# A diffusion-transformer block whose first 128 features are modulated, and multiplied, ahead of the next 128

## The chip, the core and the metric

The kernel runs on one core of a Trainium2 chip. The metric is the device time of one execution in microseconds (us). TensorE does the matrix products, VectorE and ScalarE the elementwise work, GpSimd a little of it; SyncE issues most of the loads from memory (HBM) into on-chip memory (SBUF), and products accumulate in PSUM.

## The reference, cut to what matters

One layer: adaptive norm, one combined input projection, four attention mixers, output projection, then the same norm and a SwiGLU. The change touches the way into the input projection alone:

```python
mod = (silu_c @ w_ada[l] + b_ada[l])[:, None, :]        # 2048 -> 6 * 2048
mod_c = silu_cc @ w_ada[l] + b_ada[l]                   # the same for the context
sh_a, sc_a, gt_a, sh_f, sc_f, gt_f = jnp.split(mod, 6, axis=-1)
h = rms_norm(x, g_attn[l]) * (1.0 + sc_a) + sh_a        # 256 latent tokens
hc = rms_norm(xc, g_attn[l]) * (1.0 + csc_a) + csh_a    # 256 context tokens
pl = jnp.split(h @ w_in[l], offsets, axis=-1)           # 2048 -> 4928 columns
pc = jnp.split(hc @ w_in[l], offsets, axis=-1)
```

Everything is float32. Shift and scale of one feature need its two columns of w_ada over all 2048 rows, so 128 features need 2.1 MB of that matrix.

## The kernel before, in words

A float32 product is made of three: each factor is split into a rounded part and the remainder (`whi`, `wlo` for weights, a pair in `hT` for activations), and hi*hi, hi*lo and lo*hi are added up (`mm3s`, L165 to L168). ScalarE writes the rounded part of a weight tile (L142), VectorE the remainder (L145).

The 2048 features are 16 chunks of 128, and two chunks are a "pair". The first part of the projection goes in groups of pairs, `parts = [[0], [1], [2, 3], [4, 5], [6, 7]]`: for a group, the columns of five blocks (queries of two mixers, NA_Q and GQ_Q; then NA_V, GQ_KV, NA_K) are multiplied with that group's features and added to what the groups before gave. So products can start once pair 0 is modulated.

For that, `ada_load` fetches a pair's 256 shift and 256 scale columns, 16 loads of 256 KB in rows of 1 KB, and `ada_pe` multiplies them with silu(c) on TensorE (L301): the left factor is 32 columns wide, and four blocks of 128 features (j = 0 to 3) lie side by side in four column groups of the array. The result is copied (`mvs`, L304), transposed (L307), and biases are added on VectorE (`scg`, `sha`). `modulate` forms h from the normalised, transposed tokens (`xnT`, written by `tokens_T`, transposes at L268) in three steps: h_f (L325), its rounded part on ScalarE (L330), the remainder on VectorE (L331).

The stage's order: tokens 0 and 1 (256 latent tokens) are loaded and normalised; pair 0's loads stand on SyncE's queue with the first weight tiles, NA_Q's two (`raw_q`) between them and GQ_Q's two (`raw_g`) behind; L301 and the eight `tokens_T` share TensorE; the buffers of the latent tokens are then reused for the context tokens, which GpSimd loads (`load_tokens(2)`, `(3)`, L189) when the last transpose has read them. `first_group` multiplies the query blocks, then NA_V and GQ_KV for the latent tokens (`units[:2]`), takes in the context tokens, and goes on with the rest.

Order of the instructions: Tile places each engine's instructions by a simulation of its own in which the earlier in the program goes first among those that are ready, so L301 and L268 alternate. `issue_after` (the helper `after`) adds an order on one engine. Work beside the products (the other pairs' `ada_pe`) is a set of generators in `Side`, stepped by `side.pump(cost)` when the planner's clock `now` has reached their `ready` time. For pair 1 that time is 8.0 from the start of the group.

Of the kernel before, what the change touches and what calls it, by code (L numbers as in the profile page):

```python
# [87 lines left out]
def hybrid_dit_kernel(ctx: ExitStack, tc: tile.TileContext, a, out):  # L88
# [72 lines left out]
    def mm3s(jobs, w_left=False):  # L161


        for dst, l, r, start, stop in jobs:
            pe.matmul(dst, lhsT=l[0], rhs=r[0], start=start, stop=False)  # L165
            pe.matmul(dst, lhsT=l[0 if w_left else 1], rhs=r[1 if w_left else 0], start=False, stop=False)  # L166
        for dst, l, r, start, stop in jobs:
            pe.matmul(dst, lhsT=l[1 if w_left else 0], rhs=r[0 if w_left else 1], start=False, stop=stop)  # L168

    def sub(pair, *sl):  # L170
        return pair[0][sl], pair[1][sl]
# [8 lines left out]
    def tsl(t):  # L180
        return slice(t * P, (t + 1) * P)
# [12 lines left out]
    def ada_load(pr, ks):  # L194
# [9 lines left out]
            raws.append(raw)  # L204
        return raws

    load_tokens(0)
    cc = const.tile([P, 2, KC], F32, name="cc")
    act.dma_start(cc, a["cc"].rearrange("t (p k) -> p t k", k=KC))
# [5 lines left out]


    w_in = a["w_in"]
    raws0 = ada_load(0, range(0, 12, 2))
    raw_q = stream_raw(w_in[0:2 * P, NA_Q:NA_Q + 512].rearrange("(k p) n -> p k n", p=P), [P, 2, 512])
    raws0 += ada_load(0, range(12, KC, 2))  # L220
    raw_g = stream_raw(w_in[0:2 * P, GQ_Q:GQ_Q + 512].rearrange("(k p) n -> p k n", p=P), [P, 2, 512])

    make_identity(nc, ident)
    ones = const.tile([P, 1], F32, name="ones")
# [56 lines left out]
        sp.dma_start(raw, src)  # L281
        return raw

    def ada_pe(pr, raws=None, per=4, wait=0.0):

        mv = misc()
        batches = [range(k, k + 2 * per, 2) for k in range(0, KC, 2 * per)]
        if raws is None:  # L290
            ahead = ada_load(pr, batches[0])
            yield 0.0, wait
        for i, ks in enumerate(batches):
            if raws is None:
                now, ahead = ahead, (ada_load(pr, batches[i + 1]) if i + 1 < len(batches) else None)
            else:
                now = raws[i * per:(i + 1) * per]
            for kc in range(ks[0], ks[0] + 2 * per):
                raw = now[(kc - ks[0]) // 2]
                for j in range(4):  # L300
                    pe.matmul(mv[32 * j:32 * j + 32, :P], lhsT=cs32[:, kc, :], rhs=raw[:, kc % 2, j // 2, tsl(j % 2)], start=(kc == 0), stop=(kc == KC - 1), skip_group_check=True)  # L301
            yield 0.5 * per, wait
# [12 lines left out]
        dve.tensor_tensor(out=scg[:, k2, :], in0=scg[:, k2, :], in1=col(colB[:, k2]), op=ALU.mult)  # L315
        dve.tensor_tensor(out=sha[:, k2, :], in0=cpv[:, 0], in1=col(colA[:, k2]), op=ALU.add)
        yield 0.1, 0.0

    def modulate(pr, ws_=(0, 1)):
        hf = {}  # L320
        for w in ws_:
            hf[w] = sb0.tile([P, 2, S], F32, name="h_f", bufs=2)
            for kk in range(2):
                kc = 2 * pr + kk
                dve.tensor_scalar(out=hf[w][:, kk, :], in0=xnT[pr][:, kk, w * S:(w + 1) * S], scalar1=scg[:, kc, w:w + 1], scalar2=sha[:, kc, w:w + 1], op0=ALU.mult, op1=ALU.add)  # L325
        if ws_[0] == 0:
# [11 lines left out]
        norm_tokens(t)  # L338
    for pr in range(8):
        xnT[pr] = htile(F32)  # L340
    first = ada_pe(0, raws0, 1)
    for _ in range(3):
        next(first)
    for pr in range(8):
        tokens_T(0, pr)
        if 1 < pr < 6:
            next(first)
    load_tokens(2)
    load_tokens(3)
    w_q = split(raw_q, 512)  # L350
    for _ in first:
        pass
    modulate(0, (0,))
    w_g = split(raw_g, 512)


    na_qT = kv.tile([P, 4, S], F32, name="qT", bufs=3)
# [149 lines left out]
            bias.append(b)  # L507

    def first_group():
        q_block([0], True, [w_q])  # L510
        held = {}
        for c0, units in blocks[:3]:
            held[c0] = (w_g if c0 == GQ_Q else stream_w(w_in, 0, c0, 512), units)
            if c0 == blocks[0][0]:
                behind = (newest["act"], newest["dve"])
            one_pair(held[c0], units[:2])
        with after(*behind):
            for t in (2, 3):
                norm_tokens(t)
            tokens_T(1, 0)  # L520
            modulate(0, (1,))
        for c0, units in blocks[1:3]:
            one_pair(held[c0], units[2:])
        for pr in range(1, 8):
            tokens_T(1, pr)
        c0, units = blocks[3]
        one_pair((stream_w(w_in, 0, c0, 512), None), units, True)
# [10 lines left out]
    for gi, prs in enumerate(parts):  # L538
        nxt = []
        if gi + 1 < len(parts):  # L540
            for pr in parts[gi + 1]:
                nxt.append(side.add(ada_pe(pr, wait=(3.0, 1.5, 5.5, 5.5)[gi]), lane="ada", width=1))
                if gi == 0:
                    nxt[-1]["ready"] = side.now + 8.0
        if gi == 2:
            made = prepare()
            gate_tasks = add_ada(2, 7.0, ada_raw, (0, 1))
        if gi == len(parts) - 1:
            keep(*made)
# [693 lines left out]
```

## Time and profile before

| | |
|---|---|
| time, median of 3 runs | 1356.57 us (1356.53 to 1358.23) |
| profiled execution | 1355.29 us, of which the span of its instructions is 1353.5 us |
| mean granted TensorE clock | 0.996 |
| busy: VectorE, ScalarE | 923.2 us (68%), 625.7 us (46%) |
| read from HBM | 314.56 MB, 237 GB/s over the span |

Times in the rows count from the first instruction. Engines are PE (TensorE), PEld (its weight loads), DVE (VectorE), ACT (ScalarE), POOL (GpSimd), SP (SyncE), and a row of a stretch lists them as PE, PEld, DVE, ACT, POOL. L301 is line 301. An arrow "a<-b" between tiles says that a is written from b; "[2.00 <-ACT h L330]" says that the engine sat idle for 2.00 us until that instruction released it. The ends of matrix products are modelled, so the distance between two starts tells their price. A granted clock of 1.00 is 2.4 GHz, 0.50 is 1.2 GHz.

### The profile page before, as it was taken

Reading aid. Unit: us, or ns where it says so; the run is one execution under the profiler, and the core shown is the slowest. Engines: PE = TensorE matmul, PEld = TensorE weight load, DVE = VectorE, ACT = ScalarE, POOL = GpSimd, SP = SyncE. Lnnn points to the kernel's source line nnn. Section 1 sums busy time; section 2 is a strip of 40 time slices with the busy share of each in tenths; the row PEclk is TensorE's granted clock in tenths of the full one; section 3 lists DMA queues with packets and bytes.
Section 4 is the critical chain, followed back from the end, with each engine's and each line's share of the span. In section 5 each row is a group of like instructions: output and inputs, shape, how many; then the busy total and the mean of one; then the engine's idle time right before and its main releaser. Section 6 shows DMA issues by size and latency. Waiting matters only on the chain.

```text
span 1353.5 us, 21027 instructions
## 1 busy us (share of the span) xinstructions
PE 1324.0 (98%) x7018; PEld 1077.5 (80%) x7018; DVE 923.2 (68%) x1687; ACT 625.7 (46%) x1183; POOL 99.6 (7%) x159
## 2 busy tenths in 40 slices
PE   6999999999999999999999999999999999999997
PEld 4788888778886777777888888888888888888886
DVE  4577789998679747778887954445555566556565
ACT  4532343564334435557445444444444444444453
POOL 1110000100000000000322200001001000011000
PEclk9999999999999999999999999999999999999999
DMA  9999996586687756455999855567667655676553
GB/s 367 344 356 323 322 364 220 171 268 213 198 262 262 247 166 212 135 184 164 344 368 340 307 191 192 193 196 219 210 212 228 218 193 185 203 226 224 193 178 129
DMA packets 190161, 322.29 MB, mean 238 GB/s; under 512 B 22466, under 2 KB 62436, under 8 KB 189028
## 3 DMA queue, kind: packets, MB, share of 16 engines
q1 hardware_dynamic: 177568, 285.28, 63.8%
q0 software_dynamic: 9136, 32.53, 6.5%
q10 hardware_dynamic: 3348, 3.13, 0.7%
q8 instruction: 55, 0.90, 0.3%
q14 instruction: 54, 0.44, 0.1%
HBM read 314.56 MB, written 6.31 MB: 237 GB/s over the span
## 4 chain that ended last, share of the span: by engine, by line
PE 68%; DVE 1%; ACT 1%; DMA 0%; issue 0%; POOL 0%; POOLq 0%; DVEq 0%; SPq 0%; ACTq 0%
PE acc L165 21%; PE acc L168 21%; PE acc L166 21%; PE m L862 1%; PE m L607 1%; PE m L861 1%; PE m L913 1%; PE m L897 1%; PE m L658 1%; DVE wlo L145 0%; PE m L165 0%; PE m L166 0%; PE m L168 0%; ACT whi L142 0%; DMA raw<-in_w_out_dram 0%; PE m L385 0%
## 5 line engine op out<-in xcount | busy, mean ns | idle before, releaser
L145 DVE TENSOR_TENSOR wlo<-raw,whi 128x512 fp32r<-128x512 f32 (+1 forms) x764 | 490.4, 680 | 286.0 <-ACT whi L142 281.5
L142 ACT CAST whi<-raw 128x512 fp32r<-128x512 f32 (+1 forms) x764 | 437.6, 615 | 520.2 <-PE acc L166 427.5
L165 PE MATMUL acc<-whi,h_hi 128*128 128x512 f32 x704 | 274.2, 390 | 0.7 <-ACT h_hi L1013 0.7
L166 PE MATMUL acc<-whi,h_lo 128*128 128x512 f32 x704 | 274.1, 389 | 0.4 <-DVE h_lo L1014 0.4
L168 PE MATMUL acc<-wlo,h_hi 128*128 128x512 f32 x704 | 190.8, 390 | 0.0
L165 PE MATMUL acc<-whi,h 128*128 128x512 f32 (+1 forms) x416 | 161.6, 392 | 1.2 <-ACT tok L791 0.5
L166 PE MATMUL acc<-whi,h 128*128 128x512 f32 (+1 forms) x416 | 157.1, 379 | 0.0
L168 PEld LDWEIGHTS acc<-wlo,h_hi 128*128 128x128 f32 x704 | 132.1, 188 | 28.5 <-DVE wlo L145 1.2
L165 PEld LDWEIGHTS acc<-whi,h_hi 128*128 128x128 f32 x704 | 132.2, 188 | 28.2 <-ACT h_hi L1013 1.1
L166 PEld LDWEIGHTS acc<-whi,h_lo 128*128 128x128 f32 x704 | 132.2, 188 | 28.0 <-DVE h_lo L1014 0.7
L165 PE MATMUL acc<-whi,ah 128*128 128x512 f32 (+1 forms) x364 | 139.1, 384 | 0.0
L166 PE MATMUL acc<-whi,al 128*128 128x512 f32 (+1 forms) x364 | 138.6, 382 | 0.0
L380 DVE SCALAR_TENSOR_TENSOR ada_acc<-raw,cs,ada_acc 128x512 f32<-128x512 f32 x135 | 100.9, 747 | 21.7 <-DMA raw<-in_w_ada_dram 20.2
L168 PE MATMUL acc<-wlo,h 128*128 128x512 f32 (+1 forms) x416 | 114.5, 379 | 1.1 <-DVE wlo L145 1.0
L168 PE MATMUL acc<-wlo,ah 128*128 128x512 f32 (+1 forms) x364 | 96.2, 382 | 0.0
L165 PEld LDWEIGHTS acc<-whi,h 128*128 128x128 f32 x416 | 78.0, 188 | 19.2 <-issue 3.7
L166 PEld LDWEIGHTS acc<-whi,h 128*128 128x128 f32 x416 | 78.2, 188 | 13.4 <-issue 1.2
L168 PEld LDWEIGHTS acc<-wlo,h 128*128 128x128 f32 x416 | 75.9, 188 | 16.2 <-DVE wlo L145 2.5
L165 PEld LDWEIGHTS acc<-whi,ah 128*128 128x128 f32 x364 | 68.4, 188 | 13.3
L166 PEld LDWEIGHTS acc<-whi,al 128*128 128x128 f32 x364 | 68.5, 188 | 13.1
L168 PEld LDWEIGHTS acc<-wlo,ah 128*128 128x128 f32 x364 | 67.6, 188 | 13.3
L177 POOL TENSOR_TENSOR rstd<-ms,mhalf 128x1 f32<-128x1 f32 (+2 forms) x24 | 18.1, 755 | 513.5 <-DVE ms L175 513.5
(238 smaller groups left out, 1419.8 us busy)
## 6 DMA issues: line engine op xcount, KB each, us to landing
raw<-in_ffn_wg_dram SPq DMA_DIRECT2D x176, 256.0 KB, 2.8
raw<-in_ffn_wu_dram SPq DMA_DIRECT2D x176, 256.0 KB, 3.5
raw<-in_ffn_wd_dram SPq DMA_DIRECT2D x176, 256.0 KB, 3.7
raw<-in_w_in_dram SPq DMA_DIRECT2D x144, 256.0 KB, 4.7
raw<-in_w_ada_dram SPq DMA_DIRECT2D x144, 256.0 KB, 3.4
araw<-in_w_ada_dram SPq DMA_DIRECT2D x128, 256.0 KB, 5.1
raw<-in_w_out_dram SPq DMA_DIRECT2D x64, 256.0 KB, 3.4
graw<-in_w_ada_dram POOLq DMA_DIRECT2D x32, 512.0 KB, 6.1
```

What stands on the lines that cost most here:

```text
L142: act.copy(hi, raw_)
L145: dve.tensor_tensor(out=lo, in0=raw_, in1=hi.bitcast(F32), op=ALU.subtract)
L165: pe.matmul(dst, lhsT=l[0], rhs=r[0], start=start, stop=False)
L166: pe.matmul(dst, lhsT=l[0 if w_left else 1], rhs=r[1 if w_left else 0], start=False, stop=False)
L168: pe.matmul(dst, lhsT=l[1 if w_left else 0], rhs=r[0 if w_left else 1], start=False, stop=stop)
L177: pool.tensor_tensor(out=r[:, :n], in0=v[:, :n], in1=mhalf[:, :n], op=ALU.pow)
L380: dve.scalar_tensor_tensor(out=acc_, in0=part, scalar=cs[:, 0, kc:kc + 1], in1=acc_, op0=ALU.mult, op1=ALU.add)
L607: pe.transpose(ps[:, tsl(j)], src[:, tsl(j)], ident)
L658: pe.matmul(o[:, :S], lhsT=vt(kc)[:, v0:v0 + P], rhs=pT[:, kc, :], start=(kc == 0), stop=(kc == 3))
L861: pe.matmul(sc, lhsT=ml_qT[:, h, tsl(t)], rhs=ml_kT[:, h, :], start=True, stop=False)
L862: pe.matmul(sc, lhsT=qpeT[hb, h // 2, tsl(t)], rhs=kpeT[hb, :], start=False, stop=True)
L897: pe.matmul(sc, lhsT=df_qT[hb, h, tsl(t)], rhs=df_kT[h // 2][hb, h % 2, :], start=True, stop=True)
```

## The change

Pair 0 is no longer loaded and formed by `ada_load` and `ada_pe`. `ada_load1(kc)` loads shift and scale columns of one chunk of 128 features, in 8 loads of 256 KB with rows of 512 B, and `ada_one(kc)` multiplies them in two column groups (shift, scale). The queue order becomes: 8 loads for chunk 0, its NA_Q and its GQ_Q weight tile, 8 loads for chunk 1, its two tiles. `both_blocks(kc)` multiplies one chunk with NA_Q and GQ_Q for the latent tokens; it is called for chunk 0 ahead of `ada_one(1)` in the program, and for chunk 1 in `first_group`. Chunk 0 is modulated by `modulate1(0)` as soon as its shift and scale are there. In `first_group` the context norms are ordered behind other instructions than before, and pair 1's `ada_pe` gets a later ready time (11.0 for 8.0), a longer first wait (by 5.0) and an order behind the first products of NA_V and GQ_KV.

```diff
+    def ada_load1(kc):
+        pool_, tag = ((sb0, "araw"), (opool, "o"))[kc]
+        raws = []
+        for i in range(4):
+            raw = pool_.tile([P, 2, 4, P], F32, name="araw", tag=tag, bufs=4)
+            for s in range(2):
+                sp.dma_start(raw[:, s], ada_two[:, 4 * i:4 * i + 4, s, tsl(kc)])
+            raws.append(raw)
+        return raws
...
-    raws0 = ada_load(0, range(0, 12, 2))
-    raw_q = stream_raw(w_in[0:2 * P, NA_Q:NA_Q + 512].rearrange("(k p) n -> p k n", p=P), [P, 2, 512])
-    raws0 += ada_load(0, range(12, KC, 2))
-    raw_g = stream_raw(w_in[0:2 * P, GQ_Q:GQ_Q + 512].rearrange("(k p) n -> p k n", p=P), [P, 2, 512])
+    raws0, raw_q, raw_g = [], [], []
+    for kc in range(2):
+        raws0.append(ada_load1(kc))
+        for c0, raws in ((NA_Q, raw_q), (GQ_Q, raw_g)):
+            raws += stream_raw(w_in[kc * P:(kc + 1) * P, c0:c0 + 512].unsqueeze(1), [P, 1, 512])
...
+        yield 0.0, wait + (5.0 if pr == 1 else 0.0)
         for i, ks in enumerate(batches):
+            st = after(newest["gate"]) if pr == 1 else ExitStack()
...
-    first = ada_pe(0, raws0, 1)
-    for _ in range(3):
-        next(first)
-    for pr in range(8):
+    def ada_one(kc):
+        mv = misc()
+        for i, raw in enumerate(raws0[kc]):
+            for j in range(4):
+                for s in range(2):
+                    pe.matmul(mv[32 * s:32 * s + 32, :P], lhsT=cs32[:, 4 * i + j, :], rhs=raw[:, s, j, :], start=(i + j == 0), stop=(i + j == 6), skip_group_check=True)
+            yield
+        mvs = sb0.tile([P, P], F32, name="mvs", bufs=2)
+        act.copy(mvs[0:64], mv[0:64, :P])
+        yield
+        cp = misc()
+        pe.transpose(cp[:, 0:64], mvs[0:64], ident[0:64, 0:64])
...
+    def modulate1(kc):
+        dve.tensor_scalar(out=hf0[:, kc, :], in0=xnT[0][:, kc, 0:S], scalar1=scg[:, kc, 0:1], scalar2=sha[:, kc, 0:1], op0=ALU.mult, op1=ALU.add)
+        act.copy(hT[0][0][:, kc, 0:S], hf0[:, kc, :])
+        i_a = nc.cur_bb.bb.instructions[-1]
+        dve.tensor_tensor(out=hT[0][1][:, kc, 0:S], in0=hf0[:, kc, :], in1=hT[0][0][:, kc, 0:S].bitcast(F32), op=ALU.subtract)
+        newest["chain"] = (i_a, nc.cur_bb.bb.instructions[-1])
...
+    def both_blocks(kc, w_q1, w_g1):
+        h_ = lambda t0, n: sub(hT[0], slice(None), kc, slice(t0, t0 + n))
+        for lo in range(2):
+            for h in range(4):
+                dst = q_accs[h // 2][:, h % 2 * S:(h % 2 + 1) * S]
+                l = sub(w_q1, slice(None), tsl(h))
+                for n, r in enumerate(h_(0, S)[:1] if lo else h_(0, S)):
+                    pe.matmul(dst, lhsT=l[lo], rhs=r, start=(kc == 0 and h % 2 == 0 and lo == 0 and n == 0), stop=(kc == 1 and h % 2 == 1 and lo == 1), skip_group_check=True)
+        mm3s([(g_accs[t], h_(t * P, P), w_g1, kc == 0, kc == 1) for t in range(2)])
+
+    one0, one1 = ada_one(0), ada_one(1)
+    next(one0)
+    next(one0)
+    tokens_T(0, 0)
+    next(one0)
+    tokens_T(0, 1)
+    next(one0)
+    next(one0)
+    for pr in (2, 3):
         tokens_T(0, pr)
-        if 1 < pr < 6:
-            next(first)
+    next(one0)
+    w_q = split(raw_q[:1], 512)
+    modulate1(0)
+    w_g = split(raw_g[:1], 512)
+    for pr in range(4, 8):
+        tokens_T(0, pr)
     load_tokens(2)
     load_tokens(3)
-    w_q = split(raw_q, 512)
-    for _ in first:
-        pass
-    modulate(0, (0,))
-    w_g = split(raw_g, 512)
+    both_blocks(0, w_q[0], w_g[0])
+    for _ in range(6):
+        next(one1)
+    modulate1(1)
+    w_q += split(raw_q[1:], 512)
+    w_g += split(raw_g[1:], 512)
...
     def first_group():
-        q_block([0], True, [w_q])
+        behind = newest["chain"]
+        both_blocks(1, w_q[1], w_g[1])
...
+        evacuated = nc.cur_bb.bb.instructions[-1]
+        side.pump(5.4, 2.0)
         held = {}
-        for c0, units in blocks[:3]:
...
+        for c0, units in blocks[1:3]:
+            held[c0] = (stream_w(w_in, 0, c0, 512), units)
+        for c0, units in blocks[1:3]:
             one_pair(held[c0], units[:2])
+        newest["gate"] = newest["pe"]
         with after(*behind):
-            for t in (2, 3):
-                norm_tokens(t)
+            norm_tokens(2)
+        with after(evacuated, behind[1], newest["pe"]):
+            norm_tokens(3)
             tokens_T(1, 0)
             modulate(0, (1,))
...
-                    nxt[-1]["ready"] = side.now + 8.0
+                    nxt[-1]["ready"] = side.now + 11.0
```

## Rows read from the trace of the kernel before

**Rows 1.** The page: the span, and TensorE's busy time with its share and instructions.
```profile
span 1353.5 us, 21027 instructions
...
PE 1324.0 (98%) x7018; PEld 1077.5 (80%) x7018; DVE 923.2 (68%) x1687; ACT 625.7 (46%) x1183; POOL 99.6 (7%) x159
```

**Rows 2.** Waits of TensorE over the span: who, for whom, us in total, times, longest.
```profile
PE m L239 <- DMA rowsA<-in_b_ada_dram: 8.5, 1, 8.5
PE acc L165 <- ACT h L330: 3.3, 3, 2.0
```

**Rows 3.** Timeline of TensorE: start us, us, line, op, tiles, shape, count, idle before.
```profile
20.54 1.52 PE L301 MATMUL m<-araw,cs 128*32 128x128 f32 x48
...
24.82 0.51 PE L165 MATMUL acc<-h,whi 128*128 128x256 f32 x2 [2.00 <-ACT h L330]
...
29.49 0.28 PE L165 MATMUL acc<-h,whi 128*128 128x256 f32 x1
29.61 0.28 PE L166 MATMUL acc<-h,whi 128*128 128x256 f32 x1
...
52.26 1.96 PE L301 MATMUL m<-araw,cs 128*32 128x128 f32 x64
...
58.37 0.27 PE L307 MATMUL m<-ident,mvs 128*128 128x128 f32 x1
58.57 2.60 PE L301 MATMUL m<-araw,cs 128*32 128x128 f32 x84
62.14 0.50 PE L165 MATMUL acc<-h,whi 128*128 128x256 f32 x2 [0.97 <-ACT h L330]
```

**Rows 4.** Stretches: length, busy us (x) of each engine, granted clock, DMA share, GB/s.
```profile
9.79:15.68 5.89, 5.89 (x53) 3.11 (x52) 3.00 (x8) 1.29 (x3) 0.56 (x1) 1.00 1.09 384
15.68:21.90 6.22, 6.22 (x110) 4.28 (x109) 2.19 (x4) 2.69 (x6) 1.09 (x2) 1.00 1.08 394
...
24.82:38.47 13.65, 13.47 (x61) 10.81 (x62) 6.39 (x10) 9.49 (x16) 1.11 (x2) 0.87 1.06 397
```

**Rows 5.** The first two stretches again, instructions of L301 alone.
```profile
9.79:15.68 5.89, 3.05 (x41) 1.21 (x41) 1.00 1.09 384
15.68:21.90 6.22, 3.53 (x88) 2.07 (x88) 1.00 1.08 394
```

**Rows 6.** Timelines of ScalarE and VectorE between the last L301 and the first product.
```profile
22.17 0.27 ACT L304 COPY mvs<-m 128x128 f32<-128x128 f32 x1
...
23.38 0.73 DVE L325 TENSOR_SCALAR h_f<-h,scg,sha 128x256 f32<-128x256 f32 x2
...
24.15 0.62 ACT L330 CAST h<-h_f 128x512 fp32r<-128x512 f32 x1 [0.38 <-DVE h_f L325]
```

**Rows 7.** Stretches with DMA rows of 512 B (351 us on) and of 1 KB.
```profile
351.00:353.00 2.00, 2.00 (x16) 2.00 (x15) 0.72 (x2) 0.00 (x0) 0.00 (x0) 1.00 1.04 287
31.00:36.00 5.00, 5.00 (x23) 3.63 (x22) 3.86 (x6) 5.00 (x9) 0.82 (x2) 1.00 1.09 384
```

**Rows 8.** The sixteenth load of araw alone: its issue, and the time to landing.
```profile
L203 SPq DMA_DIRECT2D araw<-in_w_ada_dram x1: 368/368/368, 15.7 to 15.7; - x1
...
DMA to landing us min/median/max: 5.4/5.4/5.4
```

**Rows 9.** GpSimd's context loads; DMA queues (packets, MB, share) at 20.8:24.4 and 24.5:30 us.
```profile
20.81 1.30 POOL L189 DMA_DIRECT2D x_t<-in_ctx_dram  x2 [9.23 <-PE m L268]
...
q1 hardware_dynamic: 833, 1.42, 103.9%
...
q0 software_dynamic: 262, 1.99, 85.5%
q1 hardware_dynamic: 326, 0.33, 16.8%
```

**Rows 10.** Stretches: granted clock after two idle times of TensorE.
```profile
26.00:29.50 3.50, 3.50 (x17) 3.50 (x18) 0.52 (x1) 1.07 (x1) 0.00 (x0) 0.51 1.02 422
...
284.00:290.00 6.00, 3.77 (x13) 2.11 (x13) 5.10 (x11) 2.98 (x8) 1.87 (x2) 1.00 1.00 342
```

More of the change, by code (lines that the diff above doesn't have):

```diff
@@ L168, in mm3s @@
             pe.matmul(dst, lhsT=l[1 if w_left else 0], rhs=r[0 if w_left else 1], start=False, stop=stop)
+        newest["pe"] = nc.cur_bb.bb.instructions[-1]
     def sub(pair, *sl):
@@ L282, in ada_raw, with ada_pe @@
         return raw
-    def ada_pe(pr, raws=None, per=4, wait=0.0):
+    def ada_pe(pr, per=4, wait=0.0):
         mv = misc()
         batches = [range(k, k + 2 * per, 2) for k in range(0, KC, 2 * per)]
-        if raws is None:
-            ahead = ada_load(pr, batches[0])
-            yield 0.0, wait
+        ahead = ada_load(pr, batches[0])
+        yield 0.0, wait + (5.0 if pr == 1 else 0.0)
         for i, ks in enumerate(batches):
[L294 to L297, printed above, removed]
+            now, ahead = ahead, (ada_load(pr, batches[i + 1]) if i + 1 < len(batches) else None)
+            st = after(newest["gate"]) if pr == 1 else ExitStack()
             for kc in range(ks[0], ks[0] + 2 * per):
@@ L301, in ada_pe @@
                     pe.matmul(mv[32 * j:32 * j + 32, :P], lhsT=cs32[:, kc, :], rhs=raw[:, kc % 2, j // 2, tsl(j % 2)], start=(kc == 0), stop=(kc == KC - 1), skip_group_check=True)
+            st.close()
             yield 0.5 * per, wait
@@ L325, in modulate @@
                 dve.tensor_scalar(out=hf[w][:, kk, :], in0=xnT[pr][:, kk, w * S:(w + 1) * S], scalar1=scg[:, kc, w:w + 1], scalar2=sha[:, kc, w:w + 1], op0=ALU.mult, op1=ALU.add)
-        if ws_[0] == 0:
+        if ws_[0] == 0 and pr:
             hT[pr] = (htile(F32R), htile(F32R))
@@ L340, in hybrid_dit_kernel @@
         xnT[pr] = htile(F32)
-    first = ada_pe(0, raws0, 1)
-    for _ in range(3):
-        next(first)
-    for pr in range(8):
-        tokens_T(0, pr)
-        if 1 < pr < 6:
-            next(first)
+    def ada_one(kc):
[10 more added lines that the diff above has]
+        pe.transpose(cp[:, 0:64], mvs[0:64], ident[0:64, 0:64])
+        cpv = cp[:, 0:64].rearrange("p (s t) -> p s t", s=2)[:, :, 0:2]
+        dve.tensor_scalar(out=scg[:, kc, :], in0=cpv[:, 1], scalar1=colA1[:, 16 + kc:17 + kc], scalar2=colB[:, kc:kc + 1], op0=ALU.add, op1=ALU.mult)
+        dve.tensor_scalar(out=sha[:, kc, :], in0=cpv[:, 0], scalar1=colA[:, kc:kc + 1], scalar2=None, op0=ALU.add)
+        yield
@@ new lines, in hybrid_dit_kernel @@
+    hT[0] = (htile(F32R), htile(F32R))
+    hf0 = sb0.tile([P, 2, S], F32, name="h_f", bufs=2)
+    def modulate1(kc):
[4 more added lines that the diff above has]
+        newest["chain"] = (i_a, nc.cur_bb.bb.instructions[-1])
@@ new lines, in hybrid_dit_kernel @@
+    q_accs, g_accs = [acc() for _ in range(2)], [acc() for _ in range(2)]
+    def both_blocks(kc, w_q1, w_g1):
[7 more added lines that the diff above has]
+        mm3s([(g_accs[t], h_(t * P, P), w_g1, kc == 0, kc == 1) for t in range(2)])
@@ L509, in first_group @@
     def first_group():
-        q_block([0], True, [w_q])
+        behind = newest["chain"]
+        both_blocks(1, w_q[1], w_g[1])
+        for hp in range(2):
+            add_up(na_qT[:, 2 * hp:2 * hp + 2, :], q_accs[hp].rearrange("p (i n) -> p i n", i=2), True)
+        for t in range(2):
+            add_up(gq_q[:, t, :], g_accs[t], True)
+        evacuated = nc.cur_bb.bb.instructions[-1]
+        side.pump(5.4, 2.0)
         held = {}
-        for c0, units in blocks[:3]:
-            held[c0] = (w_g if c0 == GQ_Q else stream_w(w_in, 0, c0, 512), units)
-            if c0 == blocks[0][0]:
-                behind = (newest["act"], newest["dve"])
+        for c0, units in blocks[1:3]:
+            held[c0] = (stream_w(w_in, 0, c0, 512), units)
+        for c0, units in blocks[1:3]:
             one_pair(held[c0], units[:2])
+        newest["gate"] = newest["pe"]
         with after(*behind):
-            for t in (2, 3):
-                norm_tokens(t)
+            norm_tokens(2)
+        with after(evacuated, behind[1], newest["pe"]):
+            norm_tokens(3)
             tokens_T(1, 0)
```

## The prediction

> **What bounds the kernel now.** I read the page first: TensorE is busy for 1324.0 of 1353.5 us [rows 1]. What is left can hardly be won in the long middle, so the next view is TensorE's waits: the first of them is the 8.5 us before the first instruction, and its wait for h from ScalarE (3.3 us in 3 pieces) is the one this change aims at [rows 2]. The timeline then shows the start: the last adaLN products (L301) run from 20.54 to 22.06, and the first product of the projection follows at 24.82 after 2.00 us of idling [rows 3]. So the question is what TensorE does before 24.82, and the table by stretch answers it: it is busy without a break from 9.79 to 21.90, with L301 and the transposes of the tokens [rows 4], while the loads keep the DMA engines full (share 1.08 to 1.09). Both are bounds at once. The sixteenth load of pair 0 is issued at 15.66 and lands 5.4 us later, at 21.0 [rows 8]; TensorE reaches its products 0.6 us after that.
>
> In the first stretch 41 instructions of L301, ten groups of four abreast, and some eleven transposes fill 5.89 us, 0.28 us a place; in the second 22 groups and 22 transposes fill 6.22 us, 0.14 a place [rows 4, 5]. I take the first stretch to be at half speed, though the record says 1.00 for both; that is an estimate from these two numbers.
>
> **The change part by part.** I follow TensorE to 38.47, where the first products of NA_V and GQ_KV end [rows 4], and then to the next group.
>
> *Narrower adaLN products.* The number of L301 instructions stays 128 (16 row chunks, 2 instructions each, 4 column groups before; the same with 2 groups and 2 halves after). Before, four run side by side: 48 in 1.52 us, 0.032 each [rows 3]. Afterwards shift and scale alone lie side by side, so two: 0.063 each, if nothing else overlaps. That adds 128 times 0.032, 4.1 us, all on TensorE and ahead of chunk 1's modulation. Bounds: 0 (row chunks that follow each other find a way to overlap) to 4.1; not below 0, since no instruction goes. I take 4.1, from the only row there is.
>
> *The block of chunk 0.* `both_blocks(0)` has 12 products of 256 columns and 6 of 512. A product of 256 columns costs 0.12 (29.49 to 29.61, [rows 3]), one of 512 twice that, an estimate: 2.9 us. It is not added work, only moved, but whatever of it TensorE does ahead of chunk 1's last L301 delays that. The order is the planner's: chunk 0's products go first when their h is ready, L301 of chunk 1 when it is not. Bounds: 0 to 2.9 us ahead; I take 1.2, less than half, because chunk 0's own wait has to pass first and loads of chunk 1 land during it.
>
> *The wait before the products.* From the last L301 (22.06) to the first product (24.82) it is 2.76 us, through the copy (0.27), transpose, biases, h_f (0.73 for both chunks) and the cast (0.62) [rows 3, 6]. For one chunk the last two halve: 2.1 us. For chunk 0 it is covered by transposes and L301 of chunk 1; for chunk 1 by the 1.7 us of chunk 0's block that are left, so some 0.4 us idle. The clock should then stay up: it fell to 0.51 after the waits of 0.4 and 2.0 us before 24.82, and stayed at 1.00 around an idle time of 2.2 us at 284 to 290 [rows 10].
>
> *Sum to 38.47.* Last L301 at 22.06 + 4.1 + 1.2 = 27.4, chunk 1's products from 29.5. Before, the stretch to 38.47 holds 24 products of 256 and 36 of 512 columns, 11.5 us by price, and takes 13.65 [rows 4], with the half clock in it. Afterwards 11.5 - 2.9 = 8.6 are left and end at 38.1: 0.4 us earlier. So the work done ahead (2.9) and the half clock saved (some 2) are paid back almost whole by the narrower products and the later start.
>
> *Loads.* Rows of 512 B moved at 287 GB/s in the query up-projection's weights, rows of 1 KB at 384 [rows 7]. A half of pair 0 (2.1 MB) takes 7.3 us instead of 5.5, both halves 3.6 more, so chunk 1's last load lands at 24.6 instead of 21.0. TensorE's 27.4 hides that in my sum; bounds 0 to 3.6. SyncE's issues for four runs a partition stay below the time that a load takes to move. The Trainium skill (DMA: Bandwidth & Descriptors, Specifications) puts the smallest transfer at line rate at 512 B; by it these loads would lose nothing and the last would land at 21.0 still. The two rows say otherwise, and my sum is the same by either, but one rival below hangs on it.
>
> *GpSimd's queue.* The context loads are issued when the last transpose has read the latent tokens, at 20.81, and none of their packets moves before 24.4 [rows 9]. The transposes end about as early as before, so I leave this at 0; its price if not is a rival.
>
> *Norms and pair 1.* Ordering the context norms behind other instructions costs nothing while the context's transposes wait for TensorE anyway. Behind a waiting Square on ScalarE stand weight casts and copies out of PSUM, and TensorE waits for those; bounds 0 to 1 us, the length of the largest boundary idle in the rows [rows 3]; I take 0. By the planner's clock pair 1's second half of L301, at 52.26 between products of NA_K before, comes behind all of NA_K. Then its copy stands in the wait before the next group, which lasts from 58.37 to 62.14 with 2.60 us of pair 2's L301 as cover and 0.97 idle [rows 3]: +0.4 (the copy and its hand-over, [rows 6]), at worst +1.1 if part of that cover has not landed.
>
> *Sum.* -0.4 + 0.4 = 0.0. On the profiled execution (1355.29, of which 1.8 lie around the span) that is 1355.3; the median stands 1.3 higher, so 1356.6. Later groups start when this one ends and no load has a time of its own there, so a shift is kept.
>
> **The rivals.**
>
> *The loads set the pace (faster).* If the narrow products overlap after all, the last L301 follows chunk 1's last load, 24.6 + 0.3. Chunk 0's block is done by then, products of chunk 1 start at 27.0 and the stretch ends at 35.6, 2.9 us earlier: 1353.7 with nothing lost at the boundary. For it: DMA is full in the same stretches. Against it: TensorE was behind its loads already.
>
> *The second wait is a bare one (slower).* If the planner sets all of chunk 0's block before chunk 1's last L301, that one ends at 22.06 + 4.1 + 2.9 = 29.1, nothing covers the 2.1 us behind it, and the clock falls as it did after 22.06: 3.5 us at 0.51 [rows 10] cost 1.7. 31.2 + 8.6 + 1.7 = 41.5, 3.0 later, with the boundary +3.4: 1360.0. It decides once chunk 1's L301 end after about 27.7 without, or 26 with, the half clock. For it: in the program that block stands ahead. Against it: loads land while chunk 0 waits.
>
> *Context loads cut in (slower).* During them SyncE's queue got 16.8% against 85.5%, 0.33 MB in 5.5 us [rows 9]. If the transposes end a microsecond earlier, their packets come while chunk 1's last loads and its two weight tiles (due at 24.6 to 25.9) are under way, and these land near 30: products of chunk 1 at 32, +2.5 to +3. The skill's rule on queues (same page, Queues, rings and completion order: each engine goes round the queues packet by packet) agrees with those shares; by its 512 B rule the loads would be through before, and this rival gone.
>
> *Nothing goes ahead.* If the planner puts the block behind chunk 1's L301, these end at 26.2, the block fills the wait, and chunk 1 starts at 29.1: 0.4 below my forecast, and not to be told from it.
>
> **How the numbers follow.** No change to speak of, with the last rival in it: 0.52, between 1354.9 and 1358.6. Loads set the pace: 0.24. Bare wait: 0.15. Context loads: 0.09. 0.2% is 2.7 us, about what can be told from no change here. So faster 0.24, same 0.52, slower 0.24. The range reaches below the fast rival's 1353.7 by the time a hidden boundary may give, to 1353.0, and to 1360.3 above the bare wait's.
>
> **What would show it.** Right: rows of L301 two abreast, 0.11 to 0.13 us apart; their last end near 27; 287 to 300 GB/s from 8 to 16 us; chunk 1's first product near 29.5; pair 1's L301 last in the group. Wrong: that product before 27.5 or after 31, a granted clock near 0.5 behind it, or context packets ahead of chunk 1's weights. If later stages differ by more than the start does, the claim that a shift is kept falls.

## The result and the profile after

The changed kernel takes 1369.54 us (median of 4 runs, 1369.12 to 1370.37) against 1356.55 of the kernel before on the same chip (1354.34 to 1358.23): a ratio of 1.0088, interval 1.0076 to 1.01, some 13 us slower. The forecast was no change, 1356.6, and its range ended at 1360.3. The profiled execution took 1369.43 us.

The page after has a span 14.1 us longer, of which TensorE is busy for 8.8 more [rows 1]. Its waits after 10 us are led by one that was not there; the second, for h, has taken the place of the 2.00 us before [rows 2, 3]. Page, then waits:

```profile
span 1367.6 us, 21035 instructions
...
PE 1332.8 (97%) x7019; PEld 1084.8 (79%) x7019; DVE 925.9 (68%) x1689; ACT 627.2 (46%) x1185; POOL 101.8 (7%) x159
```

```profile
PE m L318 <- DMA xb<-in_na_mask_dram: 3.4, 1, 3.4
PE acc L390 <- ACT h L375: 1.9, 1, 1.9
...
PE m L311 <- DMA araw<-in_w_ada_dram: 1.4, 2, 0.7
```

**The start.** In the changed kernel L358 are a chunk's products with w_ada, L364 the transpose of their sums, L390 and L165 to L168 the blocks of query columns. Timeline of TensorE (start, duration, line, tiles, shape, count, idle before it):

```profile
22.12 0.48 PE L390 MATMUL acc<-h,whi 128*128 128x256 f32 x2
...
25.13 3.69 PE L358 MATMUL m<-araw,cs 128*32 128x128 f32 x64
29.18 0.27 PE L364 MATMUL m<-ident,mvs 64*128 64x64 f32 x1 [0.36 <-ACT mvs L361]
31.31 0.50 PE L390 MATMUL acc<-h,whi 128*128 128x256 f32 x2 [1.86 <-ACT h L375]
...
41.66 3.13 PE L281 MATMUL m<-ident,x_t 128*128 128x128 f32 x27
```

Chunk 0's block starts at 22.12, and chunk 1's products stand whole behind it, from 25.13 to 28.8. Nothing is left for the 2.5 us in which ScalarE and VectorE then make h of chunk 1: TensorE idles 0.36 and 1.86 us, where 2.00 stood before [rows 3]. The stretch ends at 41.66 instead of 38.47 [rows 4]. By stretches (length, busy us (x) of PE, PEld, DVE, ACT, POOL; granted clock; DMA share; GB/s):

```profile
15.86:22.12 6.26, 6.26 (x60) 4.78 (x60) 3.48 (x8) 3.17 (x7) 0.00 (x0) 1.00 1.14 355
...
32.92:36.34 3.42, 3.42 (x13) 3.03 (x13) 1.44 (x2) 1.83 (x6) 0.56 (x1) 0.50 1.08 388
...
63.64:73.89 10.25, 8.89 (x66) 6.24 (x67) 5.00 (x11) 1.24 (x2) 9.01 (x8) 0.50 0.86 262
49.00:57.00 8.00, 8.00 (x56) 6.43 (x58) 2.84 (x5) 5.29 (x12) 0.00 (x0) 1.00 0.72 238
```

The half clock is back behind the bare wait: 0.50 from 32.92 to 36.34, as at 26 us before [rows 10]. The loads of half a row are no bound: at 355 GB/s they are through when chunk 1's products begin.

**The boundary.** The larger part comes at the end of the first group. TensorE (L311: the same products for the later pairs), then ScalarE and its DMA issues (ACTq), then SyncE's issues:

```profile
56.51 3.70 PE L311 MATMUL m<-araw,cs 128*32 128x128 f32 x128
63.63 0.48 PE L318 MATMUL m<-ident,mvs 128*128 128x128 f32 x1 [3.42 <-DMA xb<-in_na_mask_dram]
...
65.77 1.14 PE L311 MATMUL m<-araw,cs 128*32 128x128 f32 x16 [0.65 <-DMA araw<-in_w_ada_dram]
67.62 0.65 PE L311 MATMUL m<-araw,cs 128*32 128x128 f32 x8 [0.71 <-DMA araw<-in_w_ada_dram]
68.20 0.80 PE L165 MATMUL acc<-h,whi 128*128 128x256 f32 x2
```

```profile
51.15 0.40 ACTq L529 DMA_DIRECT2D xa<-in_na_bias_dram  x1
...
56.79 0.39 ACTq L532 DMA_DIRECT2D xb<-in_rope_c_dram  x1
...
58.83 0.40 ACTq L536 DMA_DIRECT2D xb<-in_gqa_gk_dram  x1
62.21 0.33 ACTq L538 DMA_DIRECT2D xb<-in_na_mask_dram  x1
...
63.31 0.27 ACT L315 COPY mvs<-m 128x128 f32<-128x128 f32 x1 [5.06 <-DMA xb<-in_gqa_gk_dram]
```

```profile
44.21 8.69 SPq L128 DMA_DIRECT2D raw<-in_w_in_dram  x5
57.22 10.99 SPq L204 DMA_DIRECT2D araw<-in_w_ada_dram  x11
```

What SyncE's issues waited for from 40 to 70 us, and, from the kernel before, SyncE's issue of the first eight loads of pair 2:

```profile
SPq L204 <- PE m L311: 4.4, 2, 4.2
```

```profile
39.70 4.70 SPq L203 DMA_DIRECT2D araw<-in_w_ada_dram  x8
```

Pair 1's products come as one run of 128 behind all of NA_K, at 56.51; before, half of them lay at 52.26 and the transpose of their sums at 58.37 [rows 3]. Two things hang on them. The copy of their sums stands on ScalarE behind a row of loads of `prepare()` (tables and biases for the mixers), which go out one by one from 51.15 to 62.58, so the transpose waits until 63.63. And pair 2's loads need the buffers that these products read: SyncE issues none of them before 57.22, after a wait of 4.2 us for L311, where the kernel before, whose pair 1 began at 38.99, issued the first eight from 39.70. The DMA share is 0.72 from 49 to 57 us (0.87 in the kernel before), and TensorE waits for two of pair 2's loads. The next group starts at 68.20 instead of 62.14 [rows 3], and the clock stays at 0.50 until 73.89. By 70 us 22.27 MB have come in, 24.96 in the kernel before.

From there the loss grows slowly: the same evacuations (sums taken out of PSUM) stand 8.9 us later than before at 67 us, 11.9 at 188, 13.9 at 434, and 13.9 at the end. The half clock fits the first rise, from 6.06 at the group's start; what holds the 5 us behind it no experiment singles out.

### The profile page after: what moved, and what is told of

It reads as the page before. It is cut to its first block, busy times and chain, and to the rows that moved or that the text cites. A ratio compares the mean times of both kernels' runs of the same rounds, so it can differ in the third digit from the quotient of the medians.

```text
span 1367.6 us, 21035 instructions
## 1 busy us (share of the span) xinstructions
PE 1332.8 (97%) x7019; PEld 1084.8 (79%) x7019; DVE 925.9 (68%) x1689; ACT 627.2 (46%) x1185; POOL 101.8 (7%) x159
## 4 chain that ended last, share of the span: by engine, by line
PE 67%; DVE 1%; ACT 1%; DMA 1%; issue 0%; POOL 0%; POOLq 0%; DVEq 0%; SPq 0%; ACTq 0%
PE acc L165 21%; PE acc L166 21%; PE acc L168 21%; PE m L932 1%; PE m L677 1%; PE m L931 1%; PE m L983 1%; PE m L967 1%; PE m L728 1%; DVE wlo L145 0%; DMA raw<-in_ffn_wg_dram 0%; PE m L165 0%; PE m L166 0%; PE m L168 0%; DMA raw<-in_w_out_dram 0%; PE m L447 0%
## 5 line engine op out<-in xcount | busy, mean ns | idle before, releaser
L165 PE MATMUL acc<-whi,h_hi 128*128 128x512 f32 x704 | 274.4, 390 | 0.7 <-ACT h_hi L1083 0.7
L168 PE MATMUL acc<-wlo,h_hi 128*128 128x512 f32 x704 | 190.6, 390 | 0.1
L165 PE MATMUL acc<-whi,h 128*128 128x512 f32 (+1 forms) x416 | 161.8, 393 | 1.3 <-ACT whi L142 0.6
L165 PEld LDWEIGHTS acc<-whi,h_hi 128*128 128x128 f32 x704 | 132.2, 188 | 28.2 <-ACT h_hi L1083 1.1
L168 PEld LDWEIGHTS acc<-wlo,h_hi 128*128 128x128 f32 x704 | 132.2, 188 | 28.2 <-DVE wlo L145 0.9
L165 PE MATMUL acc<-whi,ah 128*128 128x512 f32 (+1 forms) x364 | 139.2, 384 | 0.0
L168 PE MATMUL acc<-wlo,h 128*128 128x512 f32 (+1 forms) x416 | 114.6, 380 | 1.6 <-DVE wlo L145 1.5
L168 PE MATMUL acc<-wlo,ah 128*128 128x512 f32 (+1 forms) x364 | 96.3, 382 | 0.0
L165 PEld LDWEIGHTS acc<-whi,h 128*128 128x128 f32 x416 | 78.3, 189 | 19.2 <-issue 4.2
L168 PEld LDWEIGHTS acc<-wlo,h 128*128 128x128 f32 x416 | 76.3, 188 | 16.3 <-DVE wlo L145 2.3
L165 PEld LDWEIGHTS acc<-whi,ah 128*128 128x128 f32 x364 | 68.4, 188 | 13.2
L168 PEld LDWEIGHTS acc<-wlo,ah 128*128 128x128 f32 x364 | 67.6, 188 | 13.3
```

## Experiments

Ratios are to the kernel before, run beside each, with their 95% intervals; "the changed kernel" is 1.0088.

**1. What in the boundary costs?** First the queue of ScalarE alone: prepare()'s loads are ordered behind the copy of pair 1's sums.

```diff
         act.copy(mvs, mv[:, :P])
+        if pr == 1:
+            newest["mvs1"] = nc.cur_bb.bb.instructions[-1]
...
-            made = prepare()
+            with after(newest["mvs1"]):
+                made = prepare()
```

> The changed kernel (1369.5 us), with one order added: the seven DMA issues of prepare() on ScalarE's queue stand behind pair 1's copy (mvs), not ahead of it. Theory ScalarE's queue: TensorE's 3.42 us idle at 60.2 to 63.6 and the half clock of 10 us behind it come from that copy waiting behind these issues; so the idle time falls under 1 us, the granted clock stays at 1.00 there, and the time falls by 5 to 7 us, to 1362.5 to 1364.5. Rival, late products: what counts is that pair 1's products (L311) stand last and pair 2's loads are issued only then (57.2 us), so the next group waits for loads anyway; the time falls by 0 to 2.5 us.

1369.39 us, 1.0088 [1.0069, 1.0107]: nothing. The copy came at 59.56, 3.75 us earlier, but the wait moved on to pair 2's loads:

```profile
PE m L311 <- DMA araw<-in_w_ada_dram: 5.7, 4, 4.7
```

So the queue is one of two waits side by side, and not the one that decides. Next pair 1's timing, which the change had also moved, put back to that of the kernel before; once with the order edge (`gate`) taken out too, once with it kept:

```diff
-        yield 0.0, wait + (5.0 if pr == 1 else 0.0)
+        yield 0.0, wait
...
-                    nxt[-1]["ready"] = side.now + 11.0
+                    nxt[-1]["ready"] = side.now + 8.0
```

> The changed kernel, with pair 1's ada_pe as before the change: ready at 8.0, no extra wait of 5.0, no order behind the first products of NA_V and GQ_KV. Both theories of the boundary expect the copy to come early and the next group's wait to be covered: the idle of 3.42, the waits for loads (0.65 and 0.71) and the half clock go, and the time falls by 6 to 8.5 us, to 1361 to 1363.5. If this gives more than the run with the copy first by 2 us or over, late loads have a share of their own. If it gives under 3 us, the loss is at the start.

> The changed kernel with pair 1's timing as before (a start 8 us on, no 5 us more); the order edge behind the other group's products stays. Theory 'the late pair': the group's end is as in the kernel before (under 1.5 us of TensorE idle there, no half clock of 10 us), what is left is the start: +3 to +6 us against before, ratio 1.002 to 1.0045, some 7 us under the changed kernel. Rival 'the edge': the edge holds pair 1's products back by itself, and the time stays at the changed kernel's, ratio 1.008 to 1.009.

1363.86, 1.0039 [1.0024, 1.0054], and with the edge kept 1363.61, 1.0043 [1.0028, 1.0059]. The timing is worth some 6 us, the edge nothing. And the same timing alone put into the kernel before:

> The kernel before with one part of the change alone: pair 1's products get the later timing (a start 11 us on, 5 us more between their halves); the first pair, its loads and its order stay. Theory 'the late pair': the loss at the group's end comes from this timing by itself (pair 2's loads wait for the buffers that pair 1's products free, the copy of pair 1's sums stands late, TensorE idles 3 to 5 us there and then runs 10 us at half clock): +4 to +7 us against the kernel before, ratio 1.003 to 1.005, and the next group starts 4 to 6 us later than 62.14. Rival 'the late start': the timing hurts only since the changed start has put everything 3 us later than the loads and issues around it; alone it costs under 1.5 us, ratio 0.999 to 1.001.

1366.58, 1.0069 [1.0053, 1.0085]: 9.4 us, more than expected, by an edit that leaves the start as it was. Pair 2's first loads go out at 53.84 instead of 39.70. Its boundary repeats that of the changed kernel:

```profile
53.14 3.70 PE L301 MATMUL m<-araw,cs 128*32 128x128 f32 x128
59.31 0.47 PE L307 MATMUL m<-ident,mvs 128*128 128x128 f32 x1 [2.47 <-ACT mvs L304]
...
61.64 0.66 PE L301 MATMUL m<-araw,cs 128*32 128x128 f32 x8 [0.85 <-DMA araw<-in_w_ada_dram]
63.19 0.65 PE L301 MATMUL m<-araw,cs 128*32 128x128 f32 x8 [0.89 <-DMA araw<-in_w_ada_dram]
...
64.66 0.80 PE L165 MATMUL acc<-h,whi 128*128 128x256 f32 x2
```

The 128 products in one run, 2.47 us for the copy, then waits for pair 2's loads. The next group starts at 64.66, 2.5 us later, where 4 to 6 were expected; the rest comes behind it, with a granted clock of 0.58 from 61 to 71 us and evacuations some 7 us late at 100 to 150. "The late pair" holds and the rival (that it hurts only behind a late start) has fallen.

**2. What in the start costs?** Chunk 0's block ordered behind chunk 1's products, so that it covers the wait for their h:

```diff
-    both_blocks(0, w_q[0], w_g[0])
-    for _ in range(6):
-        next(one1)
-    modulate1(1)
+    for _ in range(4):
+        next(one1)
+    newest["one1"] = nc.cur_bb.bb.instructions[-1]
+    for _ in range(2):
+        next(one1)
+    modulate1(1)
+    with after(newest["one1"]):
+        both_blocks(0, w_q[0], w_g[0])
```

> The changed kernel, with chunk 0's block of products ordered behind chunk 1's adaLN products on TensorE, so that it fills chunk 1's wait. Theory bare wait: the block ahead (2.9 us), the 2.1 us idle behind it and 3.4 us at half clock are the start's loss; the first products of NA_V and GQ_KV end near 37.7 instead of 41.7 and the time falls by 3 to 4.5 us, to 1365 to 1366.5. Rival, the boundary decides: the next group's start hangs on ScalarE's issues and pair 1's loads, and what the start wins is waited away there; the time falls by 0 to 1 us.

1371.46, 1.0102 [1.0084, 1.012]. The start is mended (no wait ahead of chunk 1's first product, which comes at 28.99, and no half clock), yet it pays nothing: the boundary's waits grow to eat it.

```profile
PE acc L165 <- ACT h L341: 2.8, 2, 2.5
PE m L318 <- ACT mvs L315: 2.5, 1, 2.5
PE m L311 <- DMA araw<-in_w_ada_dram: 2.4, 1, 2.4
```

Then with pair 1's timing put back as well:

> The changed kernel with both repairs: chunk 0's block ordered behind chunk 1's products, so that it covers the wait for chunk 1's h, and pair 1's timing as before. Theory (the two losses are separate: the block taken ahead of chunk 1's products, some 2 to 3 us with the half clock behind it, and the late pair, some 6.5 us): the sum of the two gains, -8 to -10 us against the changed kernel, so -1 to +4 us against before, ratio 0.999 to 1.003. Rival 'a wait elsewhere': what the start gains is waited for at the group's end, as with the block behind alone; the time stays where the timing alone brings it, ratio 1.003 to 1.005.

1363.42, 1.004 [1.0026, 1.0054]: the time is the rival's, the same as with the timing alone, though the start is 2 us better. (The intervals are some 2 us wide to either side; three pairs of runs with a start 2 us better, here, above and in part 4, all show no gain.) The place is not the rival's. From 100 to 150 us the evacuations in this trace are 4.6 us later than in the kernel before, with the timing alone 7.3 or more; the gain goes at 151.70, where TensorE waits for a weight cast and the cast for its load, and behind it the two are 8.1 and 7.0 late:

```profile
151.03 1.28 ACT L142 CAST whi<-raw 128x512 fp32r<-128x512 f32 x2 [7.46 <-DMA raw<-in_w_in_dram]
```

```profile
151.70 0.50 PE L165 MATMUL acc<-whi,h 128*128 128x512 f32 x1 [1.99 <-ACT whi L142]
```

**3. A control that taught something else.** In the trace with the timing put back (the edge kept), VectorE's product of diff_l, a small parameter of a mixer, stood 8 us for a load of 1 KB at the end of ScalarE's row of loads, and TensorE 3.66 us behind it:

```profile
76.79 1.84 DVE L542 TENSOR_TENSOR xb<-xb 64x2 f32<-64x2 f32 x1 [7.98 <-DMA xb<-in_diff_l_dram]
```

```profile
79.29 0.50 PE L165 MATMUL acc<-whi,h 128*128 128x512 f32 x1 [3.66 <-DVE gq_q L478]
```

So diff_l was loaded at the start, in that kernel, in the one with the block behind, and as a control in the kernel before:

```diff
     load_tokens(1)
+    lv = const.tile([64, 4], F32, name="lv")
+    act.dma_start(lv, a["diff_l"].rearrange("t d -> d t"))
...
-        lv = xb[0:64, 832:836]
-        act.dma_start(lv, a["diff_l"].rearrange("t d -> d t"))
```

> The changed kernel with pair 1's timing as before, and the load of diff_l (1 KB in elements of 4 bytes) issued at the start of the kernel instead of behind the tables on ScalarE's queue. In the trace with the timing alone, VectorE's product of diff_l stood 8 us for that load, the evacuations behind it came late, TensorE idled 3.66 us at 79.3 and then ran 3.4 us at half clock. Theory 'in order behind a small load': without that wait 4 to 5 us come back; what is left is the start: ratio 1.001 to 1.0025. Rival 'the loads are late anyway': the weights of the second group land as late, TensorE waits for them instead (ScalarE's casts waited 12 us for a load in that stretch), and the time stays, ratio 1.0035 to 1.005.

> As the one with diff_l loaded at the start, and chunk 0's block ordered behind chunk 1's products besides, so that it covers the wait for chunk 1's h. Theory 'in order behind a small load': the start's gain of 2 us is no longer lost at 70 us: ratio 0.9995 to 1.0015, the best of the changed ones. Rival 'the loads are late anyway': 1.003 to 1.005, as without the early load of diff_l.

> The kernel before with diff_l loaded at the start and nothing else. Both theories: in its trace VectorE's product of diff_l waits 0.69 us and TensorE not at all, so no change: ratio 0.999 to 1.001. It is the control for what the early load itself costs at the start of the kernel.

1379.65 (1.0162), 1375.57 (1.0135) and the control 1372.33 (1.0109 [1.0092, 1.0126]), all above what any theory gave: 14 us for a load that nothing waits for. The control's groups from 700 to 1330 us (mean ns of one behind the busy time) show it in products that have nothing to do with that load:

```profile
L166 PE MATMUL acc<-whi,h_lo 128*128 128x512 f32 x596 | 236.1, 396 | 0.0
L165 PE MATMUL acc<-whi,h_hi 128*128 128x512 f32 x596 | 235.0, 394 | 0.0
L168 PE MATMUL acc<-wlo,h_hi 128*128 128x512 f32 x596 | 163.1, 395 | 0.0
```

The new tile lies in the pool that is laid out first, so it moves every later tile. With 1024 bytes a partition in place of 16, and nothing else changed:

```diff
-    lv = const.tile([64, 4], F32, name="lv")
+    lv = const.tile([64, 256], F32, name="lv")[:, 0:4]
```

> The kernel before with diff_l loaded at the start into a tile of 1024 bytes of each partition, where the earlier control used 16 bytes. That control took 14 us more, and its rows show why it is no test of the load: the products of 128x512 with h as the moving operand took 394 to 396 ns each in the last 600 us, against 389 in the kernel before. Theory 'the address': a small tile of 16 bytes ahead of all others puts the later tiles at other addresses, and TensorE reads them more slowly; with 1024 bytes the products take 389 ns again, ratio 0.999 to 1.001. Rival 'the load at the start': the early load of 4-byte elements or a later order of the work is what costs; ratio 1.010 again.

1358.24, 1.0007 [0.9998, 1.0017]; the same groups:

```profile
L165 PE MATMUL acc<-whi,h_hi 128*128 128x512 f32 x592 | 230.4, 389 | 0.0
L166 PE MATMUL acc<-whi,h_lo 128*128 128x512 f32 x592 | 230.3, 389 | 0.0
L168 PE MATMUL acc<-wlo,h_hi 128*128 128x512 f32 x596 | 159.3, 389 | 0.0
```

So where the later tiles lie costs the 14 us, and the load at most 2.3: TensorE's first instruction comes at 9.60 instead of 8.53 with it. The groups with other moving operands in the same window (`ah`, `al`) take 389 to 391 ns in both controls. In the kernel with block and timing mended:

> Chunk 0's block behind chunk 1's products, pair 1's timing as before and diff_l loaded at the start, its tile now of 1024 bytes. Theory 'the address': the run with the tile of 16 bytes loses some 13 us after 680 us; without that it lies where its trace was at 600 us, some 8 to 9 us less late: ratio 1.002 to 1.005, so that VectorE's wait for diff_l is not what holds the changed kernel back once the rest is mended. Rival 'in order behind a small load': 0.999 to 1.0015.

1363.68, 1.0049 [1.0034, 1.0063]: the wait for diff_l is gone, the loss is not. At 70.36 us TensorE waits 2.20 us all the same, now since VectorE's evacuation stands behind its half of a weight cast, and that behind ScalarE's, which waits for the load:

```profile
68.11 1.22 ACT L142 CAST whi<-raw 128x512 fp32r<-128x512 f32 x2 [5.81 <-DMA raw<-in_w_in_dram]
```

**4. The narrow products.** Four column groups for a chunk instead of two (the two parts added by VectorE behind the transpose):

```diff
-  pe.matmul(mv[32 * s:32 * s + 32, :P], ..., start=(i + j == 0), stop=(i + j == 6), ...)
+  pe.matmul(mv[64 * (j % 2) + 32 * s:64 * (j % 2) + 32 * s + 32, :P], ..., start=(i == 0 and j < 2), stop=(i == 3 and j > 1), ...)
...
```

> The changed kernel, with chunk 0's and chunk 1's adaLN products in four column groups (even and odd row chunks apart, added up by one reduction on VectorE). Theory narrower products: two abreast cost 3.3 us more on TensorE in all (64 in 3.69 us against 48 in 1.52), the part for chunk 1 wholly on the path; the last of them ends some 3 us earlier and the time falls by 2 to 3.5 us, to 1366 to 1367.5. Rival, loads set the pace: chunk 1's products would wait for loads that land until 22.1, or the win is waited away at the boundary; the time falls by under 1 us.

1377.24, 1.0131 [1.011, 1.0152], and together with block, timing and copy mended:

> As the one with both repairs, and besides the chunk's adaLN products in four column groups of TensorE instead of two, with the two halves added by VectorE behind the transpose, and the copies of tables and biases issued behind pair 1's copy. Theory: the narrow products cost some 3 us at the start, so this one lies 1.5 to 3.5 us under the one with both repairs: ratio 0.996 to 1.001. Rival 'loads at the end': fewer products at the start only make TensorE wait for pair 2's loads and for the context's at the group's end; no gain over both repairs, ratio 1.000 to 1.004.

1370.79, 1.0101 [1.0085, 1.0117]. Both lie above all that was expected, and both had a new tile of 16 bytes, like the control above. With padded tiles, alone and with block, timing and diff_l mended:

> The changed kernel with the chunk's products in four column groups, the new small tile of 512 bytes instead of 16 (two buffers). Without the padding this took 6 to 8 us more than the changed kernel. Theory 'the address': that was the later tiles' address; with it away, the four groups take 64 products in some 2.4 us instead of 3.7 at the start, and the time is the changed kernel's or up to 2 us less: ratio 1.007 to 1.010. Rival 'a wait elsewhere': the four groups shift the later order so that pair 2's products stand ahead of the next group, and the time stays at 1.012 to 1.014.

> All the repairs with the addresses kept: block behind chunk 1's products, pair 1's timing as before, diff_l early in 1024 bytes, four column groups with a padded tile. Theory 'separate losses, and the address': 1 to 3 us under the one without the four groups: ratio 1.000 to 1.003. Rival 'the loads are late anyway': no gain over it, 1.003 to 1.005.

1370.26, 1.0095 [1.0082, 1.0109], and 1363.96, 1.0055 [1.0036, 1.0075]. Alone, chunk 1's first product comes at 29.08 instead of 31.31; the 2.2 us are given back at 68.94, where TensorE waits 2.83 for h:

```profile
29.08 0.50 PE L391 MATMUL acc<-h,whi 128*128 128x256 f32 x2 [2.07 <-ACT h L376]
...
68.94 0.79 PE L165 MATMUL acc<-h,whi 128*128 128x256 f32 x2 [2.83 <-ACT h L341]
```

So the narrow products cost the start 2 us, and removing them wins the kernel nothing that these intervals show.

**5. Bytes, or order?** All mended versions keep some 6 us. `prepare()`'s 1 MB load of the bias is left out, in three kernels:

```diff
-        act.dma_start(xa, a["na_bias"].rearrange("t p h k -> p t h k"))
+        pool.memset(xa, 0.0)
```

> The kernel with the block behind, pair 1's timing as before and diff_l early (addresses kept), and with the 1 MB load of the neighborhood bias left out: GpSimd sets its tile to zero, so the bias is not added. Theory 'the loads are late': in this stretch the weights reach TensorE through a line of loads that a late start never wins back, and 1 MB less in it, some 3 us at 350 GB/s, lets the next group's weights land earlier: 2 to 4 us under the same kernel with the load, ratio 1.002 to 1.0035. Rival 'the order on the engines': the wait comes from the order on ScalarE, VectorE and SyncE, not from bytes: ratio stays 1.004 to 1.006.

> The changed kernel with the same load left out. Theory 'buffers, not bytes': its loads stand still from 49 to 57 us for want of buffers that pair 1's late products free, so bytes are not short there: under 2 us of gain, ratio 1.0075 to 1.009. Rival 'bytes': pair 2's loads, issued at 57, share the DMA engines with this load; without it they land earlier and 3 us come back, ratio 1.005 to 1.007.

> The kernel before with the same load left out. Theory 'the loads are late': before, the loads just keep pace and TensorE waits only 0.97 us for h at the boundary, so it gains little: 0 to 1.5 us, ratio 0.9985 to 1.000. Rival 'the loads always set the pace here': it gains the full 3 us, ratio 0.997 to 0.9985.

The mended kernel: 1361.78, 1.0028 [1.0018, 1.0038], against 1.0049 with the load. The changed kernel: 1366.51, 1.0066 [1.0053, 1.008], against 1.0088. By the ratios each wins about 3 us, give or take 2.4, and 1 MB at 355 GB/s is 3 us by estimate. So bytes look short there, in the changed kernel too, where "buffers, not bytes" had said otherwise. The waits agree: with the copy early and the bias loaded (part 1) TensorE waited 5.7 us for pair 2's loads, in the changed kernel without the bias, where the copy comes early as well, 2.0:

```profile
PE m L311 <- DMA araw<-in_w_ada_dram: 2.0, 3, 1.4
```

But the edit also takes an issue off ScalarE's queue and can change the order, as the kernel before shows: 1364.79, 1.0056 [1.0043, 1.0069], some 7 us slower with less to load. Neither theory has that. TensorE, VectorE and GpSimd at its boundary:

```profile
68.63 0.80 PE L165 MATMUL acc<-h,whi 128*128 128x256 f32 x2 [7.37 <-ACT h L330]
```

```profile
61.50 2.35 DVE L480 TENSOR_TENSOR xb<-xb 64x2 f32<-64x2 f32 x1 [5.82 <-DMA xb<-in_diff_l_dram]
63.77 0.68 DVE L145 TENSOR_TENSOR wlo<-raw,whi 128x512 fp32r<-128x512 f32 x1
...
64.56 2.11 DVE L315 TENSOR_TENSOR scg<-scg,colB 128x4 f32<-128x4 f32 x1
...
67.20 1.37 DVE L325 TENSOR_SCALAR h_f<-h,scg,sha 128x256 f32<-128x256 f32 x4
```

```profile
61.50 5.15 POOL L495 TENSOR_TENSOR xa<-xa,xb 128x1024 f32<-128x1024 f32 x2
```

With the load gone the order had VectorE's product of diff_l ahead of the weight casts and of h. It waited 5.82 us there, all of the next group's h behind it, and TensorE 7.37 us, with half clock from 64.20 to 74.44. Some 4 us of VectorE's delay are two tiny products (L480 and L315) that took 2.35 and 2.11 us beside GpSimd's, and take 0.15 and 0.16 in the kernel before. There the product of diff_l stands behind h and costs nothing. So the first boundary is held by an order that just fits, and an edit that ought to help can break it.

What is left in the mended kernel without the bias lies behind the first boundary: against the trace of the kernel before, its evacuations are 0.5 us late from 80 to 100 us, 1.4 from 100 to 150, 3.1 to 3.7 from 150 to 300 and 6 from there on. TensorE waits 1.01 and 0.72 us for weight casts at 147.52 and 148.97, as two other kernels with block and timing mended do near 151. (The kernel before was traced at 1355.29, below the medians of 1357 to 1360 beside these runs, so such offsets read some 2 us high.) No experiment was aimed at those later groups.

## Why the prediction was wrong

*"Norms and pair 1 ... +0.4, at worst +1.1"* is the step that failed, by an order of magnitude: that timing alone costs 9.4 us in the kernel before. I saw pair 1's second half move behind NA_K and priced its copy. I did not follow the buffers: both halves went there, and the loads of pair 2 wait for them on SyncE's queue, until 57.22 instead of 39.70. I had counted 2.60 us of pair 2's products as the cover of that wait; in the trace after they are what TensorE waits for. Nor did I name what stood ahead of the copy on ScalarE, though the run with the copy first shows that it does not decide.

*"The block of chunk 0 ... I take 1.2"* ahead failed too: all 3.0 us went ahead, the upper bound. The rival "the second wait is a bare one" is what happened at the start, its first product 31.2 and its end 41.5 by the working, 31.31 and 41.66 in the trace, with the half clock it asked for. That it fits so closely is partly luck: the narrow products ended at 28.8, not 29.1, and h took 2.5 us behind them, not 2.1. It had 0.15, and its 1360.0 falls short as well, since it took the boundary at +0.4.

*"No load has a time of its own there, so a shift is kept"* fell. What the start gains or loses does not reach the end as it is: 2 us won there, by two different means, came to nothing, and 1 MB less to load came to some 3 us. In this stage TensorE and the loads are tied to each other by the buffers, as SyncE's wait for L311 shows.

*Narrower products*: 64 in 3.69 us, 0.058 each, against 0.063 by the working; 3.3 us for 128 where I had 4.1. *Loads*: the half rows moved at some 355 GB/s, not 287, and hid behind TensorE as I had it. The Trainium skill (DMA: Bandwidth & Descriptors, Specifications) puts 512 B at line rate; the trace is nearer to that than to my row, but under the 384 and 394 of the whole rows [rows 4]. *GpSimd's queue* at 0 was right: the context's packets begin behind chunk 1's last load.

Of the 13 us the timing of pair 1 holds some 6 (taken out of the changed kernel) to 9 (put into the one before). The remaining 6 come with the rest of the change; the runs show that neither the bare wait, nor the narrow products, nor diff_l holds them by itself, and that they shrink by some 3 with 1 MB less to load. With block and timing mended, the traces put part of them behind 150 us. How they divide beyond that stays open. The new order of the context norms, which I had put at 0, and that of the evacuations were not varied by themselves. A version with more buffers for pair 2's loads, the direct test, was not tried, so that the buffers decide is argued from SyncE's waits and from the timing put in and taken out. No version beat the kernel before.

## What to carry to other kernels

When products are moved, follow the buffers that they free and the queue that waits to refill them, before pricing the products themselves. In a stage where loads and TensorE are both full, time won at one point can be worth nothing, as here, until the loads are earlier too; leaving out a load tests it, if the order of the rest is seen to stay. When a variant adds a tile, however small, compare the durations of products that it does not touch, or the comparison measures where the tiles lie.

## What was not expected of the hardware

- Sixteen bytes more per partition ahead of the other tiles made the products of 128x512 with h as the moving operand take 394 to 396 ns instead of 389 from 700 to 1330 us, for some 14 us in all; 1024 bytes did not. Products with `ah` and `al` kept 389 to 391. Which address is bad was not tried further.
- VectorE's product of 64x2 elements took 2.35 us when it started with GpSimd's of 128x1024 (two in 5.15 us); both began at 61.50. It took 0.15 in the kernel before, and 1.84 from 76.79 in the trace with the timing put back, beside the same two of GpSimd's (73.94 to 78.62). The Trainium skill (SBUF — State Buffer, SBUF: two separate sides) describes a pair of ports which VectorE, for an operation with two inputs in SBUF, and a GpSimd operation that reads SBUF hold one at a time, for a whole instruction. These rows agree, as does the second slow one, L315, also with both inputs in SBUF (2.11 us, 0.16 before).
- In the changed kernel the granted clock stayed at 0.50 for 10.25 us behind the 3.42 us wait that ended at 63.63, with waits of 0.65 and 0.71 in it, and for 3.42 us (32.92 to 36.34) behind the one of 1.86 that ended at 31.31.
